# Gate vectors stored as rows: a TensorE transpose and 512-byte rows in place of single-element stores

## The chip, the cores and the metric

The kernel runs on one core of a Trainium2 chip. The metric is the device time of one execution in microseconds. In the profile the engines are PE (TensorE, matrix products; PEld are its weight loads), DVE (VectorE), ACT (ScalarE), POOL (GpSimd) and SP (SyncE, which in this kernel issues all DMAs). A "q" behind a name means the engine's own instruction queue.

## What is computed

Two layers of a transformer block on 256 image tokens (x) and 256 context tokens (ctx), each 1024 wide. Every layer has a feed-forward network, a token mixing (neighbourhood attention and pooling) and a second feed-forward network. Each of them is modulated by vectors that a small matrix product makes from a conditioning vector:

```python
def mod_vectors(cvec, w_mod, b_mod):
    m = jax.nn.silu(cvec) @ w_mod + b_mod
    return jnp.split(m, N_MOD, axis=-1)        # N_MOD = 9 vectors of 1024
...
def sandwich_ffn(x, w_gate_up, w_down, g_pre, g_post, shift, scale, gate):
    h = modulate(rms_norm(x, g_pre), shift, scale)
    return x + 0.5 * gate * rms_norm(swiglu(h, w_gate_up, w_down), g_post)
...
        x = x + mx[5] * rms_norm(out_x, g[3])
```

Of the nine vectors j = 0 to 8 of a layer, three are gates: j = 2, 5 and 8. Shift and scale vectors are applied while the tokens' channels lie on the partitions; a gate multiplies a result whose tokens lie on the partitions and whose 1024 channels lie along the row, so a gate is needed as a row that is the same on all 128 partitions.

## The kernel before

**The staging.** The activations of 512 tokens stay on the chip; the weights stream in from memory in tiles of 1 MB (`raw`), and ScalarE and VectorE split each into a rounded part and a remainder (`w`), so that every product is made of three fast matmuls. A feed-forward network goes over its 22 blocks of hidden channels: for each, 24 matmuls into a bank `pg` and 24 into `pu`, then the product of the two goes into `g`, and after each group of blocks the down projection is summed in banks `pd`. PSUM has eight banks, all handed out from one pool `ps`.

**The modulation vectors.** All but the first two are made beside this work, a step at a time (`mod_steps`, line 627). Eight steps load 128 rows of the modulation weights each (`wm`, 512 KB) and let VectorE multiply and add them to an accumulator `acc` of 128 partitions by 1024 channels, one accumulator for x and one for the context (two streams; one alone for j of 5 and above in the second layer). The last step (line 646) adds over the 128 partitions: for each stream, eight DMAs of 64 KB, in pieces of 512 bytes, fold `acc` into `part` (line 652), GpSimd adds `part` down in three steps (lines 655 to 657), and a small matmul with the constant `sel` adds what is left (line 659) into a bank `pm`. That is placed in TensorE's stream between matmuls of the feed-forward network.

`finish_mod` (line 574) then has VectorE add the bias and multiply by the norm weight (`to_column`, line 560). The result `col` is a column form: element 128k + p of the vector lies on partition p, at place k, for each stream. A gate is turned to row form through memory: `finish_mod` stores it into a small tensor `grow` of 2 by 1024 in the chip's memory, in one DMA per stream,

```python
nc.sync.dma_start(out=gr[i].rearrange("(k p) -> p k", p=P), in_=r[:, i, :])
```

and much later `load_gate` (line 694) reads 1024 numbers back, copied to all 128 partitions (`gb`). In the store, neighbours on one partition lie 128 elements apart in memory, so each of the 1024 elements is a piece of its own, of 4 bytes. Both DMAs are issued by SyncE, as all others.

**What sets the order.** The program is first recorded, operation by operation, by a planner written in Python (`Recorder`, from line 186; all operations pass its line 376, and so all have that line in the profile). `price` (line 208) gives each operation a cost, `lag` (line 283) the delay between engines, and `order` (line 293) walks through a model of the engines' clocks, the DMA engines and eight DMA completion lanes, and picks at each step the operation that can start first. The order that results is what each engine executes, in order, and the waits between engines are semaphores. An operation recorded while `rec.margin` is set counts as ready that much later than its inputs: `MARGIN`, 6.0 us (line 37), is set for the small matmul of line 659. `rec.haste` lets an operation go ahead of others. A PSUM bank or a buffer is given when one is free in that model.

Of the kernel before, what the change touches and what calls it, by code (L numbers as in the profile page):

```python
# [11 lines left out]
F32 = mybir.dt.float32  # L12
F32R = mybir.dt.float32r
AF = mybir.ActivationFunctionType
# [3 lines left out]
P = 128  # L18
D = 1024
KD = D // P  # L20
# [16 lines left out]
MARGIN = 6.0  # L37
# [356 lines left out]
def tile_dit_block(  # L394
# [24 lines left out]
    rec = Recorder(PLACES, LIMITS)  # L419
    nc = rec  # L420

    def fixed(shape, name, dtype=F32):
        return rec.fixed(pool.tile(shape, dtype, name=name), shape, dtype, name)

    def bank(base="ps"):
        return rec.tile("ps", [P, 512], F32, base)
# [4 lines left out]
    def wtile(shape, base="wk", dtype=F32):  # L431
        return rec.tile("wk", shape, dtype, base)
# [7 lines left out]
    ident = rec.fixed(ident0, [P, P], F32, "ident")  # L440
# [114 lines left out]

    cols = {}
    gate_rows = {}
    first = {}

    def to_column(l, j, m, eng, streams=(0, 1)):  # L560
        n = len(streams)
        r = fixed([P, 2, KD], f"col{l}{j}")
        o = r[:, 0:n, :]
        eng.tensor_tensor(out=o, in0=m[:, 0:n, :], in1=colt[:, l, j, :].unsqueeze(1).to_broadcast([P, n, KD]), op=ALU.add)
        if j in NORM_OF:
            gn = colt[:, l, N_MOD + NORM_OF[j], :].unsqueeze(1).to_broadcast([P, n, KD])
            if j in (1, 4, 7):
                eng.scalar_tensor_tensor(out=o, in0=o, scalar=1.0, in1=gn, op0=ALU.add, op1=ALU.mult)
            else:
                eng.tensor_tensor(out=o, in0=o, in1=gn, op=ALU.mult)  # L570
        cols[(l, j)] = r
        return r

    def finish_mod(l, j, m, streams):
        r = to_column(l, j, m, nc.vector, streams)
        if j in (2, 5, 8):
            gr = rec.dram(tc.dram_tile([2, D], F32, name=f"grow{l}{j}"), F32, "grow")
            for i in streams:
                nc.sync.dma_start(out=gr[i].rearrange("(k p) -> p k", p=P), in_=r[:, i, :])
            gate_rows[(l, j)] = gr  # L580

    def first_loads():
# [44 lines left out]
    def mod_steps(l, j):  # L627
# [18 lines left out]
        def last():  # L646
            pc = bank("pm")
            for v in streams:
                part = wtile([P, KD, P], "part")
                for q in range(KD):  # L650
                    nc.sync.dma_start(
                        out=part[16 * q : 16 * (q + 1)], in_=acc[v][:, q * P : (q + 1) * P]
                    )
                n = KD // 2
                while n:
                    nc.gpsimd.tensor_add(part[:, 0:n, :], part[:, 0:n, :], part[:, n : 2 * n, :])
                    n //= 2
                rec.margin = MARGIN
                mm(pc[:, v * KD : (v + 1) * KD], part[:, 0, :], sel, True, True)
                rec.margin = 0.0  # L660
            finish_mod(l, j, pc[:, 0 : 2 * KD].rearrange("p (v k) -> p v k", v=2), streams)
# [23 lines left out]
    def need(l, j):  # L685
        while (l, j) not in cols:
            fill(1)
# [6 lines left out]
    def load_gate(l, j, streams):  # L694
        need(l, j)
        for v in streams:
            g = wtile([P, D], "gb")
            nc.sync.dma_start(out=g, in_=gate_rows[(l, j)][v].partition_broadcast(P))
            gbc[v] = g

    def power(sq, eps):
# [126 lines left out]
    def ffn(l, ff, both, nxt, rate, lead, parts):  # L828
# [54 lines left out]
        for gi, (f0, f1) in enumerate(F_GROUPS):  # L883
# [12 lines left out]
            if gi + 1 < len(F_GROUPS):  # L896
                for h in range(2):
# [13 lines left out]
                    for t in toks:  # L911
# [4 lines left out]
                        else:  # L916
                            nc.vector.tensor_add(Y[t // 2][:, t % 2, hc], Y[t // 2][:, t % 2, hc], pd[t])

        load_gate(l, 2 + 6 * ff, (0, 1) if both else (0,))
        if nxt is not None:  # L920
            need(*nxt)
# [21 lines left out]
    def token_mix(l, nxt):  # L943
# [249 lines left out]

        toks = (2, 3, 0, 1) if full else (0, 1)
        load_gate(l, 5, (0, 1) if full else (0,))
        need(*nxt)
        need(nxt[0], nxt[1] + 1)
# [154 lines left out]
```

## Time and profile before

| what | value |
|---|---|
| median of 3 runs | 1691.28 us (1691.1 to 1693.22) |
| the profiled execution, its own time | 1693.02 us |
| the profiled execution, its span (first to last instruction) | 1691.2 us |
| granted TensorE clock, mean | 0.992 |
| DMA packets under 512 bytes | 19744 of 109191 |
| gate stores (`grow<-col`) | 10 DMAs of 4.0 KB |
| gate loads (`gb_wk<-grow`) | 10 DMAs of 512.0 KB |
| gate stores: first and last issue | 108.1 and 1172.9 us |
| gate loads: first and last issue | 345.7 and 1588.5 us |

Times in the profile's views count from the start of the span. In the timeline a row is: start, duration, engine, line, operation, output<-inputs, shape, count, and in brackets how long the engine stood idle before and what ended that. In the windows view a row is: the stretch, its length, then for PE, PEld, DVE, ACT and POOL the busy time with the number of instructions, then the granted TensorE clock (1.00 is full speed), the mean busy share of the 16 DMA engines and the gigabytes per second that they moved. In the view of DMA issues the last number is the median time in us from issue to landing. In the view of waits the numbers are the total in us, how many waits, and the longest. Names such as `pm_ps` are a tile and its pool.

### The profile page before, as it was taken

How to read it: one execution, taken by the hardware profiler on the slowest of the kernel's cores; microseconds unless marked ns; L12 is line 12 of the kernel's file. 1: busy time of each engine (PE TensorE's matmuls, PEld its weight loads, DVE VectorE, ACT ScalarE, POOL GpSimd, SP SyncE). 2: the span in 40 equal slices, each digit the busy share in tenths (PEclk: the TensorE clock that was granted, in tenths of full speed). 3: DMA queues.
4: the chain of work that ended last, by engine and by line, in shares of the span. 5: the costliest groups of instructions: out<-in, count | busy, mean ns of one | idle time of the engine just before them, and what ended most of it. 6: DMA issues, size and time to landing. Idle time of an engine off the chain costs nothing.

```text
span 1691.2 us, 21873 instructions
## 1 busy us (share of the span) xinstructions
PE 1640.4 (97%) x8384; PEld 1377.1 (81%) x8384; DVE 1134.6 (67%) x1610; ACT 684.9 (40%) x1216; POOL 216.8 (13%) x264
## 2 busy tenths in 40 slices
PE   6998999999999999999999999999999999899998
PEld 4986888888878788788888888888888888779997
DVE  7977775756789779876566397633343488975664
ACT  7422322225566562222123273132222367764442
POOL 1012111101132311111110022100000022210000
PEclk9999999999999999999999999999999999999999
DMA  9477655642221435765656247632332212355551
GB/s 377 169 184 243 231 199 145 205 161 82 84 77 64 164 115 167 256 215 196 174 173 226 100 148 265 210 125 55 120 125 77 104 64 102 112 197 194 204 198 56
DMA packets 109191, 268.99 MB, mean 159 GB/s; under 512 B 19744, under 2 KB 49568, under 8 KB 97312
## 3 DMA queue, kind: packets, MB, share of 16 engines
q1 hardware_dynamic: 109088, 267.60, 46.5%
q8 instruction: 66, 1.08, 0.3%
q14 instruction: 37, 0.30, 0.1%
HBM read 251.80 MB, written 1.09 MB: 150 GB/s over the span
## 4 chain that ended last, share of the span: by engine, by line
PE 78%; DVE 7%; ACT 5%; DMA 4%; POOL 2%; issue 2%; SPq 1%; POOLq 0%; DVEq 0%; ACTq 0%
PE pd_ps L376 25%; PE pu_ps L376 22%; PE pg_ps L376 22%; PE pk_ps L376 2%; DMA wm_wk<-in_wmod_dram 2%; PE pv_ps L376 2%; ACT n_wk L376 2%; DVE w_big L376 2%; POOL rs_st L376 1%; DVE acc_wk L376 1%; PE pq_ps L376 1%; SPq L376 1%; DMA w_big<-in_wmod_dram 1%; PE pt_ps L376 1%; DMA part_wk<-acc_wk 1%
## 5 line engine op out<-in xcount | busy, mean ns | idle before, releaser
L376 DVE TENSOR_TENSOR w_big<-raw_raw,w_big 128x1024 fp32r<-128x1024 f32 x312 | 390.0, 1263 | 152.8 <-ACT w_big L376 152.2
L376 PE MATMUL pu_ps<-h_big,w_big 128*128 128x512 f32 (+1 forms) x2400 | 474.4, 351 | 0.0
L376 PE MATMUL pg_ps<-h_big,w_big 128*128 128x512 f32 (+1 forms) x2208 | 439.5, 353 | 1.4 <-ACT h_big L376 1.4
L376 ACT ACTIVATE w_big<-raw_raw 128x1024 fp32r<-128x1024 f32 x312 | 321.7, 1053 | 292.6 <-DMA raw_raw<-in_wgu_dram 130.4
L376 PEld LDWEIGHTS pu_ps<-h_big,w_big 128*128 128x128 f32 x2400 | 389.6, 188 | 62.0
L376 PE MATMUL pd_ps<-w_big,g_big 128*128 128x512 f32 x1848 | 432.7, 395 | 0.0
L376 PEld LDWEIGHTS pd_ps<-w_big,g_big 128*128 128x128 f32 x1848 | 347.5, 189 | 79.2
L376 PEld LDWEIGHTS pg_ps<-h_big,w_big 128*128 128x128 f32 x2208 | 361.7, 189 | 61.0 <-ACT h_big L376 1.8
L376 DVE SCALAR_TENSOR_TENSOR acc_wk<-wm_wk,csil,acc_wk 128x1024 f32<-128x1024 f32 x196 | 248.6, 1302 | 55.7 <-DMA wm_wk<-in_wmod_dram 55.6
L376 ACT ACTIVATE g_big<-tt_wk 128x512 fp32r<-128x512 f32 (+1 forms) x84 | 49.1, 585 | 361.2 <-DVE tt_wk L376 361.2
L376 POOL TENSOR_TENSOR part_wk<-part_wk 128x512 f32<-128x512 f32 (+2 forms) x84 | 95.8, 1140 | 539.4 <-DMA part_wk<-acc_wk 432.4
L376 POOL TENSOR_SCALAR rs_st<-sq_st 128x1 f32<-128x1 f32 x24 | 7.6, 316 | 707.7 <-ACT n_wk L376 707.6
L376 DVE TENSOR_TENSOR tt_wk<-tt_wk,pu_ps 128x512 f32<-128x512 f32 (+1 forms) x86 | 53.9, 626 | 61.7 <-PE pu_ps L376 61.3
L376 ACT ACTIVATE tt_wk<-pg_ps 128x512 f32<-128x512 f32 (+1 forms) x86 | 47.1, 548 | 118.5 <-PE pg_ps L376 100.6
L376 DVE SCALAR_TENSOR_TENSOR tt_wk<-tt_wk,pg_ps 128x512 f32<-128x512 f32 (+1 forms) x86 | 53.8, 626 | 60.5 <-ACT tt_wk L376 60.0
L376 DVE TENSOR_TENSOR g_big<-tt_wk,g_big 128x512 fp32r<-128x512 f32 (+1 forms) x84 | 56.2, 669 | 42.4 <-ACT g_big L376 42.4
L376 PE MATMUL pd_ps<-w_big,mix_big 128*128 128x512 f32 x288 | 72.2, 400 | 0.5 <-DVE mix_big L376 0.5
L376 DVE TENSOR_TENSOR y_big<-y_big,pd_ps 128x512 f32<-128x512 f32 x56 | 37.4, 681 | 43.1 <-PE pd_ps L376 43.1
L376 PEld LDWEIGHTS pd_ps<-w_big,mix_big 128*128 128x128 f32 x288 | 53.2, 191 | 12.2 <-DVE mix_big L376 1.2
L376 DVE TENSOR_SCALAR acc_wk<-wm_wk,csil 128x1024 f32<-128x1024 f32 x28 | 21.1, 772 | 52.1 <-DMA wm_wk<-in_wmod_dram 52.1
L376 PE MATMUL pk_ps<-h_big,w_big 128*128 128x512 f32 (+1 forms) x240 | 50.1, 351 | 0.0
L376 PE MATMUL pv_ps<-w_big,h_big 128*128 128x512 f32 x192 | 46.9, 396 | 0.0
(133 smaller groups left out, 1232.3 us busy)
## 6 DMA issues: line engine op xcount, KB each, us to landing
raw_raw<-in_wgu_dram SPq DMA_DIRECT2D x84, 1024.0 KB, 4.8
wm_wk<-in_wmod_dram SPq DMA_DIRECT2D x128, 512.0 KB, 6.7
raw_raw<-in_wdn_dram SPq DMA_DIRECT2D x44, 1024.0 KB, 5.1
part_wk<-acc_wk SPq DMA_DIRECT2D x224, 64.0 KB, 2.6
raw_raw<-in_wkq_dram SPq DMA_DIRECT2D x8, 1024.0 KB, 4.8
raw_raw<-in_wout_dram SPq DMA_DIRECT2D x8, 1024.0 KB, 4.9
w_big<-in_wmod_dram SPq DMA_DIRECT2D x7, 1024.0 KB, 13.2
gb_wk<-grow SPq DMA_DIRECT2D x10, 512.0 KB, 6.0
```

The lines of the kernel that those rows point to most:

```text
L376: getattr(getattr(nc, op.engine), op.method)(*[self.real(a) for a in op.args], **{k: self.real(a) for k, a in op.kw.items()})
```

## The change

Only `finish_mod` and the load in `load_gate` change. The column of a gate is transposed on TensorE, two streams in one instruction, into a PSUM bank `pr`, recorded with the 6 us margin; ScalarE copies the 16 (or, with one stream, 8) rows of 128 elements into a fixed tile `grows` that all gates share; and one DMA from SyncE stores these rows of 512 bytes each. The tensor `grow` in memory holds the same numbers in the same order, seen as 16 by 128 in place of 2 by 1024.

```diff
+    grows = fixed([2 * KD, P], "grows")
...
         if j in (2, 5, 8):
-            gr = rec.dram(tc.dram_tile([2, D], F32, name=f"grow{l}{j}"), F32, "grow")
-            for i in streams:
-                nc.sync.dma_start(out=gr[i].rearrange("(k p) -> p k", p=P), in_=r[:, i, :])
+            n = len(streams) * KD
+            gr = rec.dram(tc.dram_tile([2 * KD, P], F32, name=f"grow{l}{j}"), F32, "grow")
+            pg = bank("pr")
+            rec.margin = MARGIN
+            nc.tensor.transpose(pg[0:n, 0:P], r.rearrange("p v k -> p (v k)")[:, 0:n], ident)
+            rec.margin = 0.0
+            rows = grows
+            nc.scalar.activation(rows[0:n, :], pg[0:n, 0:P], AF.Copy)
+            nc.sync.dma_start(out=gr[0:n], in_=rows[0:n, :])
             gate_rows[(l, j)] = gr
...
             g = wtile([P, D], "gb")
-            nc.sync.dma_start(out=g, in_=gate_rows[(l, j)][v].partition_broadcast(P))
+            row = gate_rows[(l, j)][v * KD : (v + 1) * KD].rearrange("k p -> (k p)")
+            nc.sync.dma_start(out=g, in_=row.partition_broadcast(P))
```

## The prediction

> **What bounds the kernel now.** I read the page first, then TensorE's own waits, then the timeline around each of those waits, and last the DMA side of the same stretches.
>
> The head of the page gives the span and TensorE's share of it:
>
> ```profile
> span 1691.2 us, 21873 instructions
> ## 1 busy us (share of the span) xinstructions
> PE 1640.4 (97%) x8384; PEld 1377.1 (81%) x8384; DVE 1134.6 (67%) x1610; ACT 684.9 (40%) x1216; POOL 216.8 (13%) x264
> ```
>
> TensorE is the bound: 1640.4 of 1691.2 us. A change elsewhere is worth only what it takes from the other 50.8 us, or from the rate at which TensorE runs. So the question is which TensorE waits have to do with the gate stores. From the view of TensorE's waits:
>
> ```profile
> PE pm_ps L376 <- DMA part_wk<-acc_wk: 8.0, 1, 8.0
> ```
>
> It is one wait, of the small matmul that ends a modulation chunk (line 659). The timeline of TensorE puts it, and two shorter waits of the same matmul, at these places:
>
> ```profile
> 130.47 2.49 PE L376 MATMUL pd_ps<-w_big,g_big 128*128 128x512 f32 x10
> 141.00 0.59 PE L376 MATMUL pm_ps<-sel,part_wk 128*128 128x8 f32 x2 [8.04 <-DMA part_wk<-acc_wk]
> ```
>
> ```profile
> 691.64 0.39 PE L376 MATMUL pm_ps<-sel,part_wk 128*128 128x8 f32 x2 [0.60 <-POOL part_wk L376]
> ```
>
> ```profile
> 1050.18 0.39 PE L376 MATMUL pm_ps<-sel,part_wk 128*128 128x8 f32 x2 [1.87 <-POOL part_wk L376]
> ```
>
> TensorE stood still for 8.04, 0.60 and 1.87 us. What was the DMA side doing before the first? SyncE's timeline, then the landing times of what it issued from 108 to 110 us:
>
> ```profile
> 108.13 0.38 SPq L376 DMA_DIRECT2D grow<-col  x1
> 108.61 0.53 SPq L376 DMA_DIRECT2D wm_wk<-in_wmod_dram  x1
> 109.19 0.43 SPq L376 DMA_DIRECT2D grow<-col  x1
> ...
> 118.19 21.22 SPq L376 DMA_DIRECT2D part_wk<-acc_wk  x16
> ```
>
> ```profile
> wm_wk<-in_wmod_dram SPq DMA_DIRECT2D x1, 512.0 KB, 19.3
> grow<-col SPq DMA_DIRECT2D x2, 4.0 KB, 14.8
> ```
>
> Two gate stores of 4 KB take 14.8 us each to land, and the 512 KB load issued between them 19.3 us, while the page's median for such loads is 6.7:
>
> ```profile
> wm_wk<-in_wmod_dram SPq DMA_DIRECT2D x128, 512.0 KB, 6.7
> ...
> part_wk<-acc_wk SPq DMA_DIRECT2D x224, 64.0 KB, 2.6
> ...
> out_dram<-x SPq DMA_DIRECT2D x4, 256.0 KB, 2.0
> ...
> grow<-col SPq DMA_DIRECT2D x10, 4.0 KB, 11.2
> ```
>
> The store of 1024 single elements is thus the slowest small transfer of the kernel: 11.2 us for 4 KB, beside 2.0 us for 256 KB written to the same memory in rows, and 2.6 us for 64 KB in 512-byte rows. And everything queued behind it waits. The windows view, before and after the stores at 108 and 109 us, and around two later ones:
>
> ```profile
> 101.00:108.00 7.00, 7.00 (x33) 5.75 (x32) 7.00 (x9) 4.80 (x6) 0.00 (x0) 1.00 1.00 402
> 109.00:118.00 9.00, 9.00 (x40) 7.33 (x40) 9.00 (x10) 1.23 (x2) 0.00 (x0) 1.00 0.24 30
> 118.00:130.00 12.00, 12.00 (x53) 9.78 (x53) 4.22 (x5) 0.00 (x0) 0.00 (x0) 1.00 1.00 109
> 137.90:144.80 6.90, 3.80 (x10) 3.12 (x11) 6.90 (x6) 0.00 (x0) 6.40 (x4) 0.51 0.71 236
> 550.90:557.80 6.90, 6.07 (x16) 4.94 (x17) 5.83 (x17) 3.63 (x11) 2.67 (x4) 0.51 0.51 176
> 667.00:677.00 10.00, 10.00 (x45) 8.13 (x44) 10.00 (x10) 1.24 (x2) 0.00 (x0) 1.00 0.27 20
> 1032.00:1044.00 12.00, 12.00 (x53) 9.77 (x53) 7.61 (x8) 2.87 (x4) 0.00 (x0) 1.00 0.52 121
> ```
>
> The last three columns are granted clock, DMA share and GB/s. Throughput falls from 402 GB/s to 30 and 109 for some twenty microseconds, with half a megabyte and more queued; at 667 it is 20, at 1032 it is 121. So the chain of the 8.04 us is: the stores choke the DMA engines, the sixteen fold transfers (line 652) issued from 118.19 on take 21.22 us to get out of SyncE, GpSimd's adds are late, TensorE stops. The waits of 0.60 and 1.87 us end 15 and 6 us after the windows at 667 and 1032, and there too TensorE waits for GpSimd's adds.
>
> **Removed: the waits.** Would TensorE still wait at 132.96 us (141.00 less 8.04) without the choke? An unhindered run of fold transfers, and GpSimd's adds behind them:
>
> ```profile
> 165.69 4.40 SPq L376 DMA_DIRECT2D part_wk<-acc_wk  x7
> ```
>
> ```profile
> 136.18 4.77 POOL L376 TENSOR_TENSOR part_wk<-part_wk 128x512 f32<-128x512 f32 x3 [38.30 <-DVE acc_wk L376]
> ```
>
> One issue takes 4.40/7 = 0.63 us. The matmul that stopped needs the first eight: 118.19 + 8 x 0.63 = 123.2, plus 2.6 to land = 125.8, plus 4.77 of adds = 130.6. That is 2.4 us ahead of 132.96, so the whole 8.04 goes. The accumulators are done at 118.19 as it is, and can only be earlier. For the other two I have the choked windows of 10 and 12 us; a delay of that size upstream is far more than 0.60 and 1.87, so I count both as gone. Removed: 8.04 + 0.60 + 1.87 = 10.5 us.
>
> **Removed: the half clock.** From 137.9 to 144.8 us the granted clock is 0.51, against 1.00 before. TensorE ran for 3.80 us of it, and that work takes half as long at full clock: 1.9 us. Behind the two short waits I count nothing of the kind. Together 12.4 us.
>
> **Removed: DMA issues.** Ten stores become six, four issues of SyncE less, 0.38 and 0.43 us each in the rows above. That is under 2 us of a queue that mostly waits; I count nothing, and what hides it is TensorE's uninterrupted stream.
>
> **Added: six transposes on TensorE**, one for each gate, two streams together. TensorE is the path, so each counts in full. The nearest rows, from the chain:
>
> ```profile
> 43.30 0.44 PE pt_ps L376 x4
> ```
>
> ```profile
> 213.21 5.54 PE pu_ps L376 x24
> 218.75 0.12 PE pm_ps L376 x2
> 218.87 5.69 PE pg_ps L376 x24
> ```
>
> A 128x128 transpose in a row of four takes 0.44/4 = 0.11 us. A pair of small matmuls slipped into the stream costs 0.12 and makes the group behind it 5.69 - 5.54 = 0.15 longer, 0.27 in all. So one transpose lies between 0.11 and 0.27 us; I take 0.25, since each comes alone and pays its own entry. Six: 1.5 us (0.7 to 1.6).
>
> By the Trainium skill ("TensorE: Matmul & The Clock Gate", Part 4: PE-mode transpose) one of 128x128 in bf16 takes about 275 ns within a kernel; by that, an estimate, six cost 1.65 us and the sum below would be -10.75 in place of -10.9.
>
> **Added: two waits.** The transpose waits for VectorE's last step on the column. TensorE's queue is in order, so a late column stops the FFN matmuls. The planner gives the transpose the 6 us margin (line 37) that the small matmul has. Against it, the real lag in the first gate:
>
> ```profile
> 104.70 0.28 PE L376 MATMUL pm_ps<-sel,part_wk 128*128 128x8 f32 x2
> ```
>
> ```profile
> 107.95 0.16 DVE L376 TENSOR_TENSOR col<-col,colt 128x16 f32<-128x16 f32 x1
> ```
>
> The column is done 3.1 us after the matmul (108.11 - 104.98), inside the 6. I put this wait at nothing; if a column is late its price is the rival below. Then ScalarE copies 16 rows and SyncE waits for that copy where it waited for VectorE:
>
> ```profile
> L376 ACT ACTIVATE rows_wk<-pm_ps 16x128 f32<-16x128 f32 x2 | 0.5, 258 | 1.5 <-PE pm_ps L376 1.5
> ```
>
> ```profile
> SPq L376 <- DVE col L376: 45.1, 6, 15.2
> ```
>
> Six copies of 0.258 us are 1.5 us of ScalarE, which is 40% busy: nothing. SyncE already waited 45.1 us for columns in six waits, with loads queued behind, and none of the TensorE waits quoted comes from that; the cover is TensorE's 5.5 us groups. The store itself is issued later, by the margin and the copy, and loads pass it in SyncE's queue meanwhile; if it is queued too early, they stand behind it for up to the 15.2 us of the longest wait of that row, which TensorE did not notice. The new store is 16 (or 8) rows of 512 bytes, which by the rows above lands in 2.0 to 2.6 us if the rows set it and in 11.2 if its smallness does; I take the 2.6 of the row with pieces of the same size. The PSUM bank that it borrows is held for the transpose and the copy, under 1 us; nothing, or one short wait.
>
> **The sum.** -12.4 + 1.5 = -10.9 us. Against the profiled execution (1693.02 us, of which 1691.2 are span): 1682.1. That execution stands 1.7 us over the median of the runs, 1691.28; from the median it is 1680.4, my forecast. Its own range is 1677 to 1684: the transposes at either end, a rest of the small waits, and a gain or loss of a microsecond or two from operations that change places.
>
> **Rivals.** A) The planner orders the whole program anew, because six transposes and six copies come in and four issues go. Then a wait elsewhere can come or go. The largest that has nothing to do with stores:
>
> ```profile
> 551.73 0.77 PE L376 MATMUL pS_ps<-kb_big,qa_wk 128*128 128x512 f32 x1 [3.88 <-DVE qa_wk L376]
> ```
>
> With the half clock behind it (0.51 from 550.9 to 557.8, TensorE busy 6.07, so 3.0 lost) it costs 6.9 us. If it goes: 1673.5, chance 0.10. If one like it comes: 1687.3, chance 0.14. For it: the order comes from a greedy search. Against: the added operations are a tenth to a quarter of a microsecond.
>
> B) The store stays slow because it is small, or the fold transfers were late on their own: only the transposes remain, 1691.28 + 1.5 = 1692.8, chance 0.07. The 2.0 us rows of the output speak against it. The Trainium skill ("DMA: Bandwidth & Descriptors", Rules for kernel authors) speaks for it: under 64 KB a transfer is mostly overhead, and 8 KB is as far under that as 4. The trace's 64 KB at 2.6 and 4 KB at 11.2 us say that the pieces count instead.
>
> C) Slower: the transpose becomes the head-of-line wait. If VectorE is behind by more than the margin, TensorE stands; a wait of 3.88 us costs 6.9 with the half clock, as above. Two such cost 13.8 and eat the gain; it decides from there. Three of six: -12.4 + 1.5 + 20.7 = +9.8, 1701. Against: the 3.1 us lag. Chance 0.05.
>
> The forecast has 0.64. About 0.2% (3.4 us) is what a measurement can tell from no change, so the bound of faster is 1687.9. Faster: forecast, the first half of A, and most of the second, 0.84; same: the rest of it and most of B, 0.10; slower: C and a little of B, 0.06. The range 1673 to 1688 holds the forecast and both sides of A but their tails, and leaves B and C out.
>
> **What would show it.** Right: the wait of 8.0 us under the fold transfers gone, clock 1.00 from 138 to 145 us, DMA over 200 GB/s in the stretches behind the gate stores where loads are queued, stores landing in under 4 us, TensorE's busy time within 2 us of 1640, since 1.5 come in and 1.9 of half clock go. Wrong: a row of waits for the transpose, new waits in token mixing, or a row store that still lands in 9 us or more.

## The result, and the profile after

| | before | after |
|---|---|---|
| median, in runs of one chip | 1692.25 us (4 runs, 1691.1 to 1698.04) | 1678.84 us (4 runs, 1678.39 to 1679.59) |
| the profiled execution, its own time | 1693.02 us | 1679.59 us |
| its span | 1691.2 us | 1677.8 us |

The ratio is 0.9914, with a 95% interval of 0.9891 to 0.9938: the change takes off 13.4 us. Forecast were 10.9. Of all the runs below, three single executions took far longer (2477.92 us of the kernel before, 3335.81 and 4276.24 of two others) and are left out of the ratios.

The page of the changed kernel, its head and the line of DMA packets:

```profile
span 1677.8 us, 21889 instructions
...
PE 1637.7 (98%) x8390; PEld 1374.9 (82%) x8390; DVE 1132.5 (67%) x1610; ACT 689.1 (41%) x1222; POOL 214.7 (13%) x264
...
DMA packets 98953, 269.00 MB, mean 160 GB/s; under 512 B 9425, under 2 KB 39329, under 8 KB 87073
```

TensorE is busy for 1637.7 us where it was 1640.4, with six instructions more. It is without a matmul for 1677.8 - 1637.7 = 40.1 us of the span, where that was 50.8: 10.7 of the 13.4 us are idle time, and 2.7 are the same work done in less time. (A second profile of the changed kernel, from another set, has 1638.7 us busy in the same span, so some 1 us of the 2.7 is scatter.) The packets are 10,238 fewer, about the 10 x 1024 single elements.

The view of TensorE's waits, its three largest rows (total, how many, longest):

```profile
PE pt_ps L376 <- DVE n_wk L376: 9.7, 3, 8.9
PE pS_ps L376 <- DVE qa_wk L376: 5.7, 3, 3.9
PE pg_ps L376 <- ACT h_big L376: 4.0, 2, 2.7
```

The row of `pm_ps` behind the fold transfers is gone, so is the row of `pm_ps` behind GpSimd's adds (the two short waits), and no row names the transposes (`pr_ps`). What is left stands before 100 us, from 300 to 600 and from 1380 to 1500 us, where it stood before, but for a few waits of at most 0.4 us.

The same stretches of the first gate in the windows view:

```profile
101.00:108.00 7.00, 7.00 (x34) 5.72 (x33) 7.00 (x10) 4.51 (x5) 0.00 (x0) 1.00 1.03 411
109.00:118.00 9.00, 9.00 (x42) 7.23 (x41) 9.00 (x10) 1.50 (x3) 0.00 (x0) 1.00 0.44 149
118.00:130.00 12.00, 12.00 (x54) 9.80 (x53) 11.64 (x12) 3.13 (x4) 5.57 (x4) 1.00 0.50 132
130.00:140.00 10.00, 10.00 (x47) 8.15 (x46) 6.66 (x7) 3.08 (x4) 2.41 (x3) 1.00 1.04 406
```

Two columns tell it. VectorE (the third busy time) works 11.64 us of the 12 from 118 to 130, where it had 4.22: its loads arrive. And GpSimd, the fifth, has its adds (5.57 us) in that stretch, where it had none. The clock stays at 1.00. Throughput is 149 and 132 GB/s with the DMA engines half idle (0.44 and 0.50): now they wait for work, while in the kernel before, from 118 to 130 us, 109 GB/s came at a share of 1.00.

SyncE's timeline and, from the view of DMA issues, what was issued from 113 to 115 us with its landing time:

```profile
113.22 0.38 SPq L376 DMA_DIRECT2D raw_raw<-in_wdn_dram  x1
113.69 0.93 SPq L376 DMA_DIRECT2D grow<-grows  x1
114.67 0.41 SPq L376 DMA_DIRECT2D wm_wk<-in_wmod_dram  x1
117.36 10.19 SPq L376 DMA_DIRECT2D part_wk<-acc_wk  x16
```

```profile
raw_raw<-in_wdn_dram SPq DMA_DIRECT2D x1, 1024.0 KB, 5.2
wm_wk<-in_wmod_dram SPq DMA_DIRECT2D x1, 512.0 KB, 5.3
grow<-grows SPq DMA_DIRECT2D x1, 8.0 KB, 4.9
```

The load behind the store lands in 5.3 us and not in 19.3, the sixteen fold transfers leave SyncE in 10.19 us and not in 21.22.

**Where the 13.4 us lie.** Three places that both timelines of TensorE show: the small matmuls behind the first gate's chunk, the first long wait of token mixing, and a wait near the end (the row near the end has not been shown for before, so it comes first):

```profile
1421.76 0.51 PE L376 MATMUL py_ps<-ds_wk,wp_wk 128*128 128x256 f32 x2 [1.44 <-DVE ds_wk L376]
```

```profile
104.31 0.28 PE L376 MATMUL pm_ps<-sel,part_wk 128*128 128x8 f32 x2
...
541.44 3.75 PE L376 MATMUL pS_ps<-kb_big,qa_wk 128*128 128x512 f32 x8 [3.88 <-DVE qa_wk L376]
...
1409.05 0.50 PE L376 MATMUL py_ps<-ds_wk,wp_wk 128*128 128x256 f32 x2 [1.44 <-DVE ds_wk L376]
```

Against before they stand at -0.39 (104.70), -10.29 (551.73) and -12.71 us (1421.76); the end of the span at -13.4. So 0.4 us are gained in start-up, ahead of any gate store; 9.9 over the first two gates; 2.4 over the other four; and 0.7 in the stretch from 1421.76 (1409.05) us on, behind the last gate store. The first and the last of these are no more than scatter: in ten other profiled executions of the kernels below the first place lies between 103.44 and 105.19 us (104.88 in the kernel with ten row stores), and the last stretch takes 268.5 to 269.2 us, where it takes 269.4 before and 268.8 after.

### The profile page after: what moved, and what is told of

Same layout as the page of the kernel before. It is cut to its first block, busy times and chain, and to the rows that moved or that the text cites. A ratio compares the mean times of both kernels' runs of the same rounds, so it can differ in the third digit from the quotient of the medians.

```text
span 1677.8 us, 21889 instructions
## 1 busy us (share of the span) xinstructions
PE 1637.7 (98%) x8390; PEld 1374.9 (82%) x8390; DVE 1132.5 (67%) x1610; ACT 689.1 (41%) x1222; POOL 214.7 (13%) x264
## 4 chain that ended last, share of the span: by engine, by line
PE 85%; DVE 5%; ACT 5%; POOL 2%; issue 1%; DMA 1%; SPq 0%; DVEq 0%; POOLq 0%; ACTq 0%
PE pd_ps L376 26%; PE pu_ps L376 25%; PE pg_ps L376 25%; PE pk_ps L376 2%; PE pv_ps L376 2%; ACT n_wk L376 2%; DVE w_big L376 1%; POOL rs_st L376 1%; PE pq_ps L376 1%; DMA w_big<-in_wmod_dram 1%; PE pt_ps L376 1%; ACT w_big L376 1%; PE po_ps L376 1%; ACT sx_wk L376 1%; ACT yg_wk L376 1%
## 5 line engine op out<-in xcount | busy, mean ns | idle before, releaser
L376 PEld LDWEIGHTS pk_ps<-h_big,w_big 128*128 128x128 f32 x240 | 37.7, 188 | 5.1
## 6 DMA issues: line engine op xcount, KB each, us to landing
w_big<-in_wmod_dram SPq DMA_DIRECT2D x7, 1024.0 KB, 11.7
```

The source lines that it names most:

```text
L376: getattr(getattr(nc, op.engine), op.method)(*[self.real(a) for a in op.args], **{k: self.real(a) for k, a in op.kw.items()})
```

## The experiments

Each kernel was timed beside the kernel before on the same chip, and its ratio is to that. The median of the kernel before was 1693.4 to 1695.69 us in these sets.

### The changed kernel once more

In another set the changed kernel took 1679.82 us beside 1693.4: 0.9919 (0.9902 to 0.9935).

> The changed kernel itself once more, on the same chip as the two others of this call, so that they can be held against it: 1678.8, within 1.5; 0.991 of the kernel before.

The gain is the same in both sets.

### Is it the number of DMA issues?

```diff
-            nc.sync.dma_start(out=gr[0:n], in_=rows[0:n, :])
+            for i in range(len(streams)):
+                nc.sync.dma_start(out=gr[i * KD : (i + 1) * KD], in_=rows[i * KD : (i + 1) * KD, :])
```

> The changed kernel, but each gate's rows are stored by one DMA per stream: ten row stores in place of six, as many issues as before. If the shape of the pieces is what counts, nothing is lost: 1678.8 us, within 1.5. If part of the gain came from SyncE's four issues less or from fewer DMA completions to wait for, some of the 13.4 us comes back: 1681 or more.

Measured: 1679.32 us beside 1694.06, ratio 0.9908 (0.9893 to 0.9923). With ten issues, as before, the whole gain is there. SyncE's four issues less were rightly counted at nothing.

### Do the transposes alone change the order to the better?

The transposes and copies stay, their rows are read by nothing, and the gate is stored from the column in single elements.

```diff
-            nc.sync.dma_start(out=gr[0:n], in_=rows[0:n, :])
+            for i in streams:
+                nc.sync.dma_start(out=gr[i * KD : (i + 1) * KD].rearrange("k p -> p k"), in_=r[:, i, :])
```

> The changed kernel with all six transposes and copies kept, but the copied rows are not used: the store goes element by element from the column, one DMA per stream, as before the change. If the pieces are the cause, the three waits of TensorE and the half clock return and the transposes come on top: 1692.3 plus 0.7 to 1.6, so about 1693.5. If the gain came from another order of the program around the transposes, it stays at about 1679 to 1683.

Measured: 1696.35 us beside 1694.06, 1.0011 (0.9999 to 1.0023). The timeline and the view of TensorE's waits of this kernel have the old wait back:

```profile
140.46 0.59 PE L376 MATMUL pm_ps<-sel,part_wk 128*128 128x8 f32 x2 [8.17 <-POOL part_wk L376]
```

```profile
PE pm_ps L376 <- POOL part_wk L376: 10.8, 3, 8.2
```

The transposes bring nothing by themselves. The gain comes with the form of the store.

### Is it the late gate, or the store in the way of others?

Rows are stored and used as in the change; beside them the old single elements go to a tensor that nothing reads.

```diff
+            junk = rec.dram(tc.dram_tile([2, D], F32, name=f"junk{l}{j}"), F32, "junk")
+            for i in streams:
+                nc.sync.dma_start(out=junk[i].rearrange("(k p) -> p k", p=P), in_=r[:, i, :])
```

> The changed kernel, and beside each row store the old element stores to a tensor in memory that nothing reads. Nothing waits for these stores, so only what they do to the DMA engines and to SyncE's queue can cost. If choked DMA engines are the cause, most of the 13.4 us comes back: 1688 to 1694. If what counted was how long the store of the gate itself takes to land, nothing comes back: 1679 to 1681.

Measured: 1694.03 us beside 1694.06, 0.9994 (0.9977 to 1.001). All of the gain is gone, with waits as before:

```profile
141.41 0.60 PE L376 MATMUL pm_ps<-sel,part_wk 128*128 128x8 f32 x2 [9.30 <-POOL part_wk L376]
```

Nobody waits for that store. Its harm is to the transfers around it. The gate's own row store lands late here too (the first in 18.8 us), but the first gate is read back only at 351.6 us, and TensorE's long wait is for GpSimd's adds: it isn't the late gate.

### What makes the store slow: size, count, or place?

Two kernels put a chain of transfers behind the end of the changed kernel, each waiting for the one before it, so their totals (1753.09 and 1738.65 us) mean nothing. The first varies size and form:

```diff
+    put(flat[0 : 16 * P].rearrange("(k p) -> k p", p=P), src[0:16, 0:P])
+    elements(8)
...
+    elements(4)
+    elements(16)
+    put(J[:, :, 0], src[:, 0:8])
...
+    put(J[:, :, 0:16], s3[:, :, 0:16])
...
+    nc.sync.dma_start(out=X[0].rearrange("p (a c) -> p a c", a=KD)[:, :, 0], in_=src[:, 0:8])
```

> The changed kernel with a chain of thirteen transfers behind the end of the work, each waiting for the one before: rows of 512 bytes; 1024 elements twice, 512, and 2048; 1024 elements that lie 1 KB apart; 128 pieces of 32 bytes; 1024 pieces of 64, 256 and 512 bytes; a 512 KB load; 1024 elements into the chip's own buffer; and last 1024 elements with a 512 KB load right behind. Only the landing times are of interest; the total is longer by their sum. If each single-element write costs by itself, landing grows with the count: about 2 us plus 7 us for each 1024, so 5.5, 9 and 16 us for 512, 1024 and 2048, the rows land in 2 to 2.6 us, and the load behind the elements lands about as late as they do. If the 11 us were only the loads in front of the stores, all element stores land in 2 to 4 us here. If the number of pieces counts and not their size, 1024 pieces of 64, 256 and 512 bytes land as late as the elements. If it is memory off the chip that is slow with single elements, the same 1024 elements into the chip's own buffer land in under 4 us.

From the view of DMA issues, each asked for by its own stretch of time: 16 rows of 512 bytes, 1024 neighbouring elements, 512 of them, 1024 elements 1 KB apart, 1024 pieces of 64 bytes at the same distance, and 1024 elements into SBUF (the chip's own buffer), 512 bytes apart on each partition:

```profile
J<-x SPq DMA_DIRECT2D x1, 8.0 KB, 1.9
J<-x SPq DMA_DIRECT2D x1, 4.0 KB, 10.3
...
J<-x SPq DMA_DIRECT2D x1, 2.0 KB, 9.0
J<-x SPq DMA_DIRECT2D x1, 4.0 KB, 3.0
J<-x SPq DMA_DIRECT2D x1, 64.0 KB, 2.4
...
x<-x SPq DMA_DIRECT2D x1, 4.0 KB, 2.3
```

The second and the fourth row are 1024 pieces of 4 bytes each, in another order. Alone, with nothing queued, they take 10.3 us side by side (8.5 and 9.5 in two repeats) and 3.0 us when 1 KB lies between them. Into SBUF as many, set apart too, take 2.3 us; neighbours were not tried there. So neither the small size nor the count is the price; it is neighbours in the chip's memory written one by one. Half as many cost 9.0, not the 5.5 expected of a price for each element. Last in this chain a 512 KB load was issued right behind such a store, at 1737.42 us: its data still move at 119 GB/s from 1749 to 1750 us, where alone such a load lands in 3.2 us.

The Trainium skill ("DMA: Bandwidth & Descriptors", Rules for kernel authors) says that an access strided in its last dimension becomes one descriptor per element, and advises making it contiguous. The trace agrees with the advice, but 3.0 us for as many pieces set apart show that one piece per element is not what costs the 10.3 here.

The second kernel varies the distance of 1024 elements, then tries other forms:

```diff
+    for c in (1, 2, 4, 8, 16, 32, 64, 128, 1):
+        o = J[0 : KD * P * c].rearrange("(k p c) -> p k c", p=P, c=c)
+        nc.sync.dma_start(out=o[:, :, 0], in_=src[:, 0:KD])
```

> The changed kernel with a chain of stores behind the end of the work, each waiting for the one before: 1024 single elements that lie 4, 8, 16, 32, 64, 128, 256 and 512 bytes apart in memory, then 4 bytes apart again; 128 elements 4 bytes apart; 1024 elements of which each partition writes eight neighbours; and 1024 pieces of 8 and of 32 bytes without a space between. Only the landing times are of interest. If writes to one stretch of memory go one after the other, the landing falls from about 9 us with the distance and is about 3 us once each element has a stretch to itself; the distance at which it stops falling is the stretch. By the count of writes to a stretch, 128 elements 4 bytes apart take as long as 1024, about 9 us, and 1024 pieces of 32 bytes under 4 us. If only the distance between pages of 512 bytes or 1 KB counted, all up to 256 bytes land in 8 us or more. If the number of elements counted, 128 would land in under 4 us.

The issues in order, from the same view: 4, 8, 16, 32 bytes apart, then 512, then 4 again, and 128 elements 4 bytes apart:

```profile
J<-x SPq DMA_DIRECT2D x1, 4.0 KB, 10.6
J<-x SPq DMA_DIRECT2D x1, 4.0 KB, 4.2
J<-x SPq DMA_DIRECT2D x1, 4.0 KB, 3.1
J<-x SPq DMA_DIRECT2D x1, 4.0 KB, 2.9
...
J<-x SPq DMA_DIRECT2D x1, 4.0 KB, 2.4
J<-x SPq DMA_DIRECT2D x1, 4.0 KB, 10.3
J<-x SPq DMA_DIRECT2D x1, 0.5 KB, 7.1
```

All of these keep the order of the gate's elements. The cost falls from 10.6 to 3.1 us between 4 and 16 bytes, and hardly from there on. 128 neighbours take 7.1, neither the 9 or so nor the less than 4 that the two ways of counting expected. Of the other forms, 1024 pieces of 8 bytes without a space take 4.3 us, and 1024 neighbours of which each partition writes eight in a row take 6.5; for the 32-byte pieces the trace has no landing. So the distance is shown as the cause; why neighbours are slow is not.

### The same elements set apart, in the kernel

The unread store of above, its elements 1 KB apart:

```diff
+            junk = rec.dram(tc.dram_tile([2, KD, P, 2 * P], F32, name=f"junk{l}{j}"), F32, "junk")
+            for i in streams:
+                nc.sync.dma_start(out=junk[i].rearrange("k p c -> p k c")[:, :, 0], in_=r[:, i, :])
```

> The changed kernel with an unused element store beside each row store, 1024 single elements in each as in the run with element stores to an unread tensor, but each element 1 KB from the next in memory. If it is the neighbours written one by one that choke the DMA engines (alone, 1024 neighbours landed in 10.3 and 8.5 us, 1024 elements 1 KB apart in 3.0), nothing comes back: 1679 to 1681. If single elements choke as such, most of the 13.4 us comes back, as with neighbours: 1688 to 1694.

Measured: 1680.46 us beside 1695.69, 0.9899 (0.9881 to 0.9918). Its windows view and, from the view of issues, the landing of these stores:

```profile
109.00:118.00 9.00, 9.00 (x42) 7.23 (x41) 9.00 (x10) 1.50 (x3) 0.00 (x0) 1.00 0.61 150
```

```profile
junk<-col SPq DMA_DIRECT2D x10, 4.0 KB, 3.8
```

Against the kernel with neighbouring elements (0.9994), ten stores with the same number and size of pieces cost nothing that can be told, and they land in 3.8 us, where the neighbouring ones took 11.9. It is the distance of the elements that decides, in the kernel as alone.

### Which gate carries the gain?

Two kernels from the kernel before, with both forms of the store and a test for the gate; (0, 2) is the first one. In the first kernel it alone keeps the elements, in the second it alone is stored in rows.

```diff
+            if (l, j) == (0, 2):
+                gr = rec.dram(tc.dram_tile([2 * KD, P], F32, name=f"grow{l}{j}"), F32, "grow")
+                for i in streams:
+                    nc.sync.dma_start(out=gr[i * KD : (i + 1) * KD].rearrange("k p -> p k"), in_=r[:, i, :])
+            else:
...
```

> The changed kernel, but the first gate (layer 0, j = 2) is stored as before, element by element from its column and without a transpose; the other five go as rows. If the 8.04 us wait and the half clock behind it belong to this gate's stores alone, they come back and nothing else: 1678.8 + 9.9 = 1688.7, within 1.5. If the cost is spread over all gates, a sixth comes back: about 1681.

```diff
+            if (l, j) != (0, 2):
...
```

> The other way round: only the first gate goes as rows, the other five are stored element by element. If the first gate carries the gain, 1692.3 - 9.9 + 0.2 = 1682.6, within 1.5, with the two short waits near 690 and 1050 us still there. If the gain needs all six, it stays above 1688.

Measured: with the first gate by elements 1691.07 us beside 1695.69, 0.9967 (0.9951 to 0.9983); with the first gate alone by rows 1677.98 (three executions, 1677.83 to 1682.74), 0.9897 (0.9874 to 0.992). The long wait stands in the first kernel. The second is faster than expected, and the two short waits, which were to stay, show next to nothing in its timeline, although eight element stores are left and choke as before (28 GB/s from 655 to 665 us, and a 512 KB load behind them lands in 12.5). That was a miss:

```profile
139.90 0.60 PE L376 MATMUL pm_ps<-sel,part_wk 128*128 128x8 f32 x2 [7.70 <-POOL part_wk L376]
```

```profile
679.11 0.39 PE L376 MATMUL pm_ps<-sel,part_wk 128*128 128x8 f32 x2
...
1035.61 0.28 PE L376 MATMUL pm_ps<-sel,part_wk 128*128 128x8 f32 x2
```

The first gate brings nearly all of what these intervals can tell. The two shares (0.33 and 1.03%) are more together than the 1.01% that the changed kernel with harmless extra stores (above) brought in the same set, though the intervals are wide. That they aren't prices that add up is told by the waits: in the five profiles with rows, and no neighbouring elements, at the later gates the short waits are gone; of the seven with neighbouring elements there six have at least one, and this one has none. Those stores are needed for the short waits, but don't make them by themselves.

### Is a store harmless if it stands elsewhere?

The kernel before, its first gate's two stores held back by 30 us or more (they went out at 137.77 and 179.54 us):

```diff
+            rec.margin = 30.0 if (l, j) == (0, 2) else 0.0
             for i in streams:
                 nc.sync.dma_start(out=gr[i].rearrange("(k p) -> p k", p=P), in_=r[:, i, :])
+            rec.margin = 0.0
```

> The kernel before the change, all stores element by element, but the first gate's two stores are held back by 30 us in the planner, so that the sixteen fold transfers that TensorE waited for go out ahead of them. If the choke costs only what is queued close behind it and needed soon, the 8.04 us wait and its half clock go though the stores are as slow as ever: 1692.3 - 9.9 = 1682.4, within 2. If an element store costs TensorE its time wherever it stands, nothing changes: 1691 to 1695.

Measured: 1694.69 us beside 1693.4, 1.0012 (0.9996 to 1.0028). This was a miss. I held that a choke costs only what stands close behind it. The wait at 132 us is gone, but TensorE's timeline has a new one, and VectorE's timeline says from where:

```profile
295.54 1.87 PE L376 MATMUL pd_ps<-w_big,g_big 128*128 128x512 f32 x3 [12.26 <-ACT g_big L376]
```

```profile
286.52 1.42 DVE L376 TENSOR_SCALAR acc_wk<-wm_wk,csil 128x1024 f32<-128x1024 f32 x2 [22.40 <-DMA wm_wk<-in_wmod_dram]
```

VectorE stood 22.40 us for a load behind the second gate's element stores, and the FFN's products queued behind it on VectorE came late. The kernel before has that wait too, as its timeline shows:

```profile
282.85 1.42 DVE L376 TENSOR_SCALAR acc_wk<-wm_wk,csil 128x1024 f32<-128x1024 f32 x2 [16.69 <-DMA wm_wk<-in_wmod_dram]
```

There TensorE had no wait behind it. It had already lost 10 us at 132 and asked for the products that much later. One could read it that the second choke was covered by the first, but the kernel with the first gate alone by rows speaks against that. It has the second gate's element stores, no first choke and no wait at 132, TensorE is at the same place (its down projection starts at 264.08 us there and at 263.62 here), and TensorE is busy for 10.00 of every 10 us from 250 to 300. VectorE's wait is there, but shorter:

```profile
267.67 2.06 DVE L376 TENSOR_SCALAR acc_wk<-wm_wk,csil 128x1024 f32<-128x1024 f32 x2 [11.73 <-DMA wm_wk<-in_wmod_dram]
```

What differs is how late VectorE comes to it. The last step on the second gate's column, first in that kernel, then with the first stores late:

```profile
249.04 0.17 DVE L376 TENSOR_TENSOR col<-col,colt 128x16 f32<-128x16 f32 x1
```

```profile
260.76 0.18 DVE L376 TENSOR_TENSOR col<-col,colt 128x16 f32<-128x16 f32 x1
```

By then VectorE has waited 28.6 us (from 110 us on) for loads of modulation weights here, and 12.0 there. So the late stores of the first gate put VectorE 11.7 us behind, and with that the second choke stopped TensorE.

A last kernel adds to this one rows for the second gate alone, (0, 5):

```diff
+            if (l, j) != (0, 5):
...
+                rec.margin = 30.0 if (l, j) == (0, 2) else 0.0
...
+            else:
...
```

> The kernel with all stores element by element and the first gate's two held back by 30 us, in which TensorE's wait of 8 us had gone from 133 us and one of 12.26 us had come at 283 us; and now the second gate (layer 0, j = 5), whose stores stood 15 us ahead of that new wait, goes as rows. If the second gate's own choke made the 12.26 us, both waits are gone and it is 1680 to 1684. If the first gate's late stores made it, by what they took from VectorE earlier, the wait at 283 stays at 8 us or more and it is 1690 to 1695.

Measured: 1687.25 us beside 1694.37, 0.9953 (0.994 to 0.9966), between the two expectations. The wait of 12.26 us is gone; in its place TensorE's waits show

```profile
PE pr_ps L376 <- DVE col L376: 4.3, 1, 4.3
```

This is rival C's head-of-line wait: VectorE, late by the first gate's stores, has the column of the second ready at 260.9 us again, 4.3 us after the transpose's turn. So neither choke makes the 12.26 us alone: the second one with VectorE in time costs TensorE nothing, and VectorE's lateness without the second choke costs 4.3 us at the transpose, with a granted clock of 0.59 behind it (261 to 268 us), and no wait at 283.

### Is it the queue, or the engines behind it?

The kernel before, the element stores issued by ScalarE:

```diff
-                nc.sync.dma_start(out=gr[i].rearrange("(k p) -> p k", p=P), in_=r[:, i, :])
+                nc.scalar.dma_start(out=gr[i].rearrange("(k p) -> p k", p=P), in_=r[:, i, :])
```

> The kernel before the change, with the element stores issued by ScalarE in place of SyncE, so that they stand in another queue than the loads and the fold transfers. If the DMA engines or the memory are what is choked, the loads suffer as before: 1690 to 1696, and loads issued just behind the first stores land in over 12 us. If only SyncE's own queue was blocked, the loads pass the stores and the waits go: 1678 to 1682.

Measured: 1682.35 us beside 1693.4, 0.9934 (0.9919 to 0.9949), between the expectations. The issues from 107 to 117 us and the windows of this kernel:

```profile
raw_raw<-in_wdn_dram SPq DMA_DIRECT2D x1, 1024.0 KB, 9.3
wm_wk<-in_wmod_dram SPq DMA_DIRECT2D x1, 512.0 KB, 10.9
grow<-col ACTq DMA_DIRECT2D x2, 4.0 KB, 9.8
```

```profile
109.00:118.00 9.00, 9.00 (x41) 7.33 (x40) 9.00 (x10) 1.23 (x2) 0.00 (x0) 1.00 0.30 15
118.00:130.00 12.00, 12.00 (x53) 9.78 (x53) 8.27 (x9) 3.01 (x4) 2.39 (x2) 1.00 0.73 199
```

The stores are as slow as ever, 9.8 us, and the loads beside them take 9.3 and 10.9 us where 5.2 and 5.3 are possible. But they take no 19.3, VectorE gets 8.27 us of work from 118 to 130, and the long wait is gone. In the same set the changed kernel was 1679.82 (above). So of some 13.6 us, 11 are gained by not standing behind the store in one queue, and some 2.5 are left to sharing what lies behind both queues. The waits agree: the two short ones are left, with 1.06 and 2.25 us, and the six transposes (0.7 us, below) are not in this kernel, which makes 2.6.

The Trainium skill ("DMA: Bandwidth & Descriptors", Issuing engines are not separate DMA queues) says that transfers run on the same 16 engines whoever issues them, so that a second issuer saves only the time of issuing. The loads' 9.3 and 10.9 us agree that the stores still get in their way; that the time falls by 11 us doesn't fit the rest of it.

## Why the prediction was right

**The long wait** was right in mechanism and size: 8.04 us are gone, and so is the half clock behind them (1.00 from 130 to 140 and from 138 to 145 us). In the profiles of the kernels with neighbouring elements written in SyncE's queue at the first gate's place, the wait is there with 7.70 to 9.30 us; with rows, with late stores or with stores in ScalarE's queue it is not. Over the first two gates the sum said -8.04 - 1.9 + 2 x 0.25 = -9.4, and the timelines give -9.9. (Of the row that it read, 14.8 us is the median of two stores that took 9.2 and 20.4; nothing in the sum hangs on it.)

**The two short waits** are gone as well, 0.60 and 1.87 us. Their size was right, but that each is the price of the stores ahead of it was luck in part: with the first gate alone by rows they went too, with those stores in place. Over the other four gates the sum said -0.60 - 1.87 + 4 x 0.25 = -1.5; the timelines give -2.4.

**The transposes** were the term that was mis-sized. The chain of the changed kernel around the first one:

```profile
108.14 5.04 PE pg_ps L376 x22
113.18 0.11 PE pr_ps L376
113.29 0.46 PE pg_ps L376 x2
113.75 5.54 PE pu_ps L376 x24
```

It costs 0.11 us, as do the five others in the chain, and the matmuls around it keep their pace: 5.04/22 = 0.23 ahead of it and 0.46/2 = 0.23 behind. In the timeline its row lasts 0.27 us, but the next matmul's row starts 0.03 us after it, so the duration is not the cost. That "each comes alone and pays its own entry" was wrong; it pays none. Six cost 0.7 us, the low end that I gave, not 1.5. That is 0.8 of the 2.5 us by which the sum was short.

**What was not in the sum** is the 0.4 us in start-up and the 0.7 behind the last gate store, which are scatter, as shown above. Together with the transposes that is 1.9 of the 2.5; the rest, 0.6, lies near the waits and is not explained. All of it is small beside the scatter of the kernel before, whose medians run from 1692.25 to 1695.69 us over the sets: that the sum came within 2.5 us of the measured gain tells no more than that its large terms were right.

**The waits added** cost nothing, as said: no transpose waited, the copies are off the path. The lag could have failed: in the kernel with the late first gate and rows for the second it did, by 4.3 us. So rival C has a real mechanism, whose condition (VectorE far behind) the changed kernel doesn't meet.

**Rival A** did not happen: the wait of 3.88 us stands at 541.44 as it stood at 551.73. **Rival B** is refuted by 1.9 us for 16 rows alone, against 10.3 for half the bytes in elements. But my reason for setting it aside, that "the pieces count", was only half of it: 1024 pieces of 4 bytes set apart take 3.0 us. The pieces count when they are neighbours.

**Of the signs**, three came out otherwise. The first row store landed in 4.9 us and the second in 7.4, not under 4 and not in the 2.6 that I took; ahead of the first a load of 1 MB was issued, 0.47 us before it, and nobody waits for it. And the stretches behind the gate store have 149 and 132 GB/s, not over 200, for little more was queued; once it was, at 130 us, it came to 406. And TensorE's busy time is 1637.7 us, 2.3 under 1640 and not within 2 (1638.7 in the second profile): the transposes brought in 0.7 us and not 1.5.

**What was right for less reason than I thought**: three waits were added up as if each had its own cause and price. The runs show them coupled. A choke that TensorE doesn't feel may still put VectorE behind, and then a later one stops TensorE that would have cost nothing alone, as the late store showed. And the two shorter waits came and went with the order of the transfers: gone with the first gate alone by rows, there, with 1.06 and 2.25 us, with the elements in ScalarE's queue.

## What to carry to other kernels

Look at the landing time per kilobyte of the small transfers, and at what is queued behind them: ten stores of 4 KB that nobody waits for cost over 14 us here (1694.03 for 1679.32 us) through the loads behind them. If a vector has to be turned and stored in the chip's memory, turn it first, so that no neighbours are written one by one; a transpose in TensorE's stream costs 0.11 us. Elements set apart also landed fast, from 16 bytes on alone and at 1 KB beside the kernel's work; as the gate's own store that was not tried. Before a choke is priced alone, ask how far behind it leaves the engine that feeds the busiest one, and what hits that engine next.

## What was not expected of the hardware

- 1024 single elements written to the chip's memory land in 10.6 us at 4 bytes' distance (8.5 to 10.3 in repeats), 4.2 at 8, 3.1 at 16, 2.9 at 32 and 2.4 at 512; 128 at 4 bytes take 7.1; 1024 into SBUF, 512 bytes apart, take 2.3.
- The harm of such a store depends on the queue: loads behind it in the same one land after up to 19.3 us, beside it in another queue after 9.3 and 10.9, behind a store of rows after 5.3.
- Kernels with these stores scatter: the kernel before ranged from 1689.87 to 1698.47 us in one set (13 executions), in which the changed kernel ranged from 1679.4 to 1680.23 (4 executions). Why was not tried.
